# A LoRA kernel: the small matrix A loaded as it lies in DRAM, on the scalar queue, and put in its place by selection matmuls

## The chip, the cores and the metric

The kernel runs on one core of one Trainium2 chip. The metric is device time in microseconds (us) of one execution; lower is better. Executions of the kernel before stayed within about 0.3% in the first runs, so differences of a few tenths of a per cent are hard to tell. A profiled execution gives a span that is about 1.9 us shorter than its time, because the time also holds what lies outside the traced instructions.

## The reference

```python
def setup_inputs():
    batch, seq, d_model, r = 16, 512, 768, 16
    # x: [16, 512, 768], A: [768, 16], B: [16, 768], all float32; scale = 0.5

def reference(x, A, B, scale):
    lora = np.matmul(np.matmul(x, A), B)
    return (x + scale * lora).astype(np.float32)
```

x is 25.2 MB and is read once; the output is 25.2 MB and is written once. A and B are 48 KB each. So nearly all traffic is x and the output, and A and B are a setup matter.

## The kernel before

x is cut into eight groups of 1,024 rows. A group is one load and one store of 3 MB, with 24,576 contiguous bytes on each of 128 partitions. There are six buffers of that size, so the last two loads wait for the first two stores. Each group is cast to 16 bits (ScalarE, "ACT"), transposed in 32x32 blocks (VectorE, "DVE"), multiplied by A (TensorE, "PE"), scaled into a block-diagonal tile (ACT), multiplied by B (PE), and added to x in place (DVE).

A has to stand in a layout that fits the transposed blocks: partition i holds rows 64b + 2i and 64b + 2i + 1 for each of 12 blocks b. The kernel before lets the DMA build that layout, in pieces of 128 bytes. One matmul with `rep` then copies the 32 partitions of A onto four partition quarters.

```python
    def sync_program():
        load(0)                       # ... moved ahead of the opening barrier
        nc.sync.dma_start(
            out=a32.rearrange("i (b r) -> i b r", b=NB),
            in_=A.rearrange("(b i q) r -> i b (q r)", i=Q, q=2),
        ).then_inc(a_in, 16)
        nc.sync.dma_start(out=b32, in_=B).then_inc(b_in, 16)
        for g in range(1, X_BUFS):
            load(g)
        for g in range(NG - 1):
            nc.sync.wait_ge(added, 4 * (g + 1) + 2)
            # ... store group g; after the second store, loads 6 and 7
    # ...
    def vector_program():
        nc.vector.wait_ge(pool_done, 2)
        nc.vector.tensor_copy(out=a16, in_=a32)._wait_ge(a_in, 16).then_inc(setup_dve, 1)
        nc.vector.tensor_copy(out=b16[0:R, :], in_=b32)._wait_ge(b_in, 16).then_inc(setup_dve, 1)
        for a in range(NQ):           # four copies from PSUM into a_diag
            # ...
        nc.vector.tensor_copy(out=b_rep, in_=b_ps)._wait_ge(setup_pe, 2).then_inc(added, 2)
        turn(0, 0, G // 2)._wait_ge(ready, 1)      # the first transpose
        # ...
    def tensor_program():
        nc.tensor.matmul(a_ps, rep, a16, start=True, stop=True)._wait_ge(setup_dve, 1).then_inc(setup_pe, 1)
        # ...
        with nc.tensor.Fori(0, NG) as g:           # the loop over groups
            wait = nc.tensor.lower_val(g + 2)      # waits against a register's value
            # ...
```

## Time and profile before

| | before |
|---|---|
| time, median of 4 runs | 123.52 us (123.25 to 123.57) |
| span of the profiled run | 121.3 us |
| share of the DMA engines' span in use | 97.8% |
| busiest compute engine | DVE, 69% |
| last add ends / last store is issued | 105.6 / 106.1 us |

The page of the kernel before, its rows for the DMA engines: the first row is the busy share of the 16 DMA engines in 40 equal slices of the span, in tenths (9 is 90% or more), the second what they moved, then come the packets and the queue (packets, MB, share of 16 engines).

```profile
DMA  7999999999999999999999999999999999999991
GB/s 227 421 392 419 397 478 413 397 478 421 397 478 405 413 470 413 413 454 430 413 446 438 413 438 446 413 438 438 421 438 438 413 446 438 413 446 438 413 454 73
DMA packets 2736, 50.43 MB, mean 416 GB/s; under 512 B 672, under 2 KB 672, under 8 KB 688
q1 hardware_dynamic: 2736, 50.43, 97.8%
```

No slice between the first and the last has any room. The packet records of the trace say the same: a packet of 24,576 bytes takes 912 ns, so 16 engines stream 431 GB/s. Of the 672 packets under 512 bytes, 384 are A's pieces of 128 bytes and 288 are the completion writes of 18 transfers on 16 engines.

The timeline of the kernel before, DVE's first and last instructions (start us, duration us, engine, line, operation, out<-in, shape, count, idle time before and what ended it):

```profile
10.79 0.35 DVE L175 CAST a_73<-a_70 32x384 f16<-32x384 f32 x1 [10.79 <-DMA a_70<-in_A_dram]
11.10 0.55 DVE L178 CAST b_74<-b_71 16x768 f16<-16x768 f32 x1
11.72 2.26 DVE L183 CAST a_diag<-lora_ps_78 32x384 f16<-32x384 f32 x4
13.99 0.96 DVE L188 CAST b_rep<-lora_ps_79 128x768 f16<-128x768 f32 x1
14.87 3.43 DVE L166 STREAM_TRANSPOSE xt<-xh_66 128x1536 uint32<-128x1536 uint32 x2
...
103.87 1.75 DVE L197 TENSOR_TENSOR x_61<-x_61,lora_ps_79 128x1536 f32<-128x1536 f32 x1
```

The same timeline, the sync queue's issues ("SPq") of the first and the last two stores:

```profile
33.47 0.35 SPq L116 DMA_DIRECT2D out_dram<-x  x1
...
96.11 0.33 SPq L116 DMA_DIRECT2D out_dram<-x  x1
106.12 0.33 SPq L253 DMA_DIRECT2D out_dram<-x_61  x1
```

DVE waits for A until 10.79 us, does the setup, and starts the first transpose at 14.87 us. The chain of waits on the page of the kernel before names DVE as the main part of what ended last:

```profile
DVE 44%; PE 22%; DMA 13%; ACT 6%; SPq 1%; issue 1%
```

That chain is true, and it is still not what bounds the kernel. It ends with the last add; the last store is then issued at 106.12 us, and by the packet records the engines finish the store before it only at 111.7 us (quickest engine) to 112.8 us (slowest). The last store waits in the queue. The two readings differ by the slack that compute has.

### The profile page before, as it was taken

To read this page: it belongs to the slowest core of one execution; us is meant where nothing else is said; L and a number is where in the kernel's file an instruction comes from. 1 tells how busy PE (TensorE), PEld (TensorE's weight loads), DVE (VectorE), ACT (ScalarE), POOL (GpSimd) and SP (SyncE) were. 2 spreads that over 40 slices of the span, in tenths; PEclk is the share of its full clock that TensorE was granted. 3 is DMA by queue.
4 is the path that set the end of the run, shared out by engine and by line. 5 is a ranking of instruction groups with operands and counts; after the bars stand their busy time and mean duration, and the time that the engine had idled before them with its cause. 6 is when DMAs were issued, how large, how long until landed. Compare 5 with 4: busy or idle time off the path is not lost.

```text
span 121.3 us, 888 instructions
## 1 busy us (share of the span) xinstructions
PE 52.1 (43%) x323; PEld 30.6 (25%) x323; DVE 84.2 (69%) x48; ACT 55.9 (46%) x42; POOL 4.9 (4%) x9
## 2 busy tenths in 40 slices
PE   0003109576944684294375449437446745000000
PEld 0000006331622362172144227216213522000000
DVE  0004990299959999999999999999999639800000
ACT  4005929989159719917943395992400220000000
POOL 6900000000000000000000000000000000000000
PEclk9999999965699999999999999999999999975555
DMA  7999999999999999999999999999999999999991
GB/s 227 421 392 419 397 478 413 397 478 421 397 478 405 413 470 413 413 454 430 413 446 438 413 438 446 413 438 438 421 438 438 413 446 438 413 446 438 413 454 73
DMA packets 2736, 50.43 MB, mean 416 GB/s; under 512 B 672, under 2 KB 672, under 8 KB 688
## 3 DMA queue, kind: packets, MB, share of 16 engines
q1 hardware_dynamic: 2736, 50.43, 97.8%
HBM read 25.26 MB, written 25.17 MB: 416 GB/s over the span
## 4 chain that ended last, share of the span: by engine, by line
DVE 44%; PE 22%; DMA 13%; ACT 6%; SPq 1%; issue 1%
DVE xt L166 19%; PE y_ps L224 16%; DMA x_61<-in_x_dram 13%; DVE x_61 L197 8%; DVE x L197 5%; PE lora_ps_79 L238 5%; ACT xh_67 L143 4%; DVE x_65 L197 3%; DVE x_63 L197 3%; DVE x_64 L197 3%; DVE x_62 L197 3%; ACT y_diag L154 1%; PE lora_ps_78 L238 1%; SPq L111 1%; SPq L107 0%
## 5 line engine op out<-in xcount | busy, mean ns | idle before, releaser
L224 PE MATMUL y_ps<-xt,a_diag 128*128 128x256 f16 x192 | 24.8, 287 | 5.8 <-DVE xt L166 5.8
L238 PE MATMUL lora_ps_78<-b_rep,y_diag 128*128 128x512 f16 (+1 forms) x64 | 14.1, 346 | 27.9 <-ACT y_diag L154 14.1
L154 ACT ACTIVATE y_diag<-y_ps 32x256 f16<-32x256 f32 x32 | 12.0, 375 | 28.0 <-PE y_ps L224 27.7
L224 PEld LDWEIGHTS y_ps<-xt,a_diag 128*128 128x128 f16 x192 | 19.3, 101 | 11.6 <-DVE xt L166 6.5
L166 DVE STREAM_TRANSPOSE xt<-xh_67 128x3072 uint32<-128x3072 uint32 x4 | 13.5, 3378 | 5.9 <-ACT xh_67 L143 5.1
L238 PE MATMUL lora_ps_79<-b_rep,y_diag 128*128 128x512 f16 (+1 forms) x64 | 14.4, 351 | 6.1 <-DVE x_61 L197 1.7
L143 ACT CAST xh_66<-x 128x3072 f16<-128x3072 f32 (+1 forms) x3 | 10.7, 3604 | 10.3 <-DMA x<-in_x_dram 10.3
L166 DVE STREAM_TRANSPOSE xt<-xh_66 128x3072 uint32<-128x3072 uint32 (+1 forms) x5 | 13.6, 2728 | 1.8 <-PE y_ps L224 1.8
L238 PEld LDWEIGHTS lora_ps_78<-b_rep,y_diag 128*128 128x128 f16 x64 | 5.1, 100 | 35.8 <-issue 16.6
L143 ACT CAST xh_67<-x_61 128x6144 f16<-128x6144 f32 x2 | 10.6, 5312 | 2.3 <-DMA x_61<-in_x_dram 2.3
L238 PEld LDWEIGHTS lora_ps_79<-b_rep,y_diag 128*128 128x128 f16 x64 | 5.9, 103 | 13.2 <-DVE x_61 L197 2.4
L197 DVE TENSOR_TENSOR x_61<-x_61,lora_ps_78 128x1536 f32<-128x1536 f32 x4 | 7.0, 1741 | 2.8 <-PE lora_ps_78 L238 2.8
L175 DVE CAST a_73<-a_70 32x384 f16<-32x384 f32 x1 | 0.3, 349 | 10.8 <-DMA a_70<-in_A_dram 10.8
L197 DVE TENSOR_TENSOR x_61<-x_61,lora_ps_79 128x1536 f32<-128x1536 f32 x4 | 7.0, 1744 | 0.0
L197 DVE TENSOR_TENSOR x<-x,lora_ps_79 128x1536 f32<-128x1536 f32 x4 | 7.0, 1741 | 0.0
L197 DVE TENSOR_TENSOR x<-x,lora_ps_78 128x1536 f32<-128x1536 f32 x4 | 6.9, 1729 | 0.0
L143 ACT CAST xh_66<-x_62 128x6144 f16<-128x6144 f32 x1 | 5.3, 5313 | 0.4 <-DMA x_62<-in_x_dram 0.4
L143 ACT CAST xh_67<-x_63 128x6144 f16<-128x6144 f32 x1 | 5.3, 5314 | 0.0
L143 ACT CAST xh_67<-x_65 128x6144 f16<-128x6144 f32 x1 | 5.3, 5313 | 0.0
L143 ACT CAST xh_66<-x_64 128x6144 f16<-128x6144 f32 x1 | 5.3, 5312 | 0.0
L209 PE MATMUL lora_ps_78<-a_73,rep 32*128 32x384 f16 x1 | 0.5, 496 | 11.2 <-DVE a_73 L175 11.2
L197 DVE TENSOR_TENSOR x_62<-x_62,lora_ps_79 128x1536 f32<-128x1536 f32 x2 | 3.5, 1742 | 0.0
(23 smaller groups left out, 35.5 us busy)
## 6 DMA issues: line engine op xcount, KB each, us to landing
x<-in_x_dram SPq DMA_DIRECT2D x2, 3072.0 KB, 12.5
x_61<-in_x_dram SPq DMA_DIRECT2D x2, 3072.0 KB, 15.2
out_dram<-x SPq DMA_DIRECT2D x2, 3072.0 KB, 19.1
out_dram<-x_61 SPq DMA_DIRECT2D x2, 3072.0 KB, 15.8
x_62<-in_x_dram SPq DMA_DIRECT2D x1, 3072.0 KB, 22.7
x_63<-in_x_dram SPq DMA_DIRECT2D x1, 3072.0 KB, 29.6
x_64<-in_x_dram SPq DMA_DIRECT2D x1, 3072.0 KB, 36.3
x_65<-in_x_dram SPq DMA_DIRECT2D x1, 3072.0 KB, 43.1
```

The lines of the kernel that those rows point to most:

```text
L111: nc.sync.dma_start(out=b32, in_=B).then_inc(b_in, 16)
L143: i = nc.scalar.copy(out=xh[g % 2][:, rows, :], in_=xs[g % X_BUFS][:, rows, :])
L154: i = nc.scalar.mul(out=y_diag[q, :, q], in_=y_ps[q, :, :], mul=sc)
L166: i = nc.vector.transpose(out=xt[:, rows, :].rearrange("p s w -> p (s w)"), in_=xh[g % 2][:, rows, :].rearrange("p s d -> p (s d)").bitcas ...
L175: nc.vector.tensor_copy(out=a16, in_=a32)._wait_ge(a_in, 16).then_inc(setup_dve, 1)
L197: nc.vector.tensor_tensor(out=rows, in0=rows, in1=lora_ps[n % 2], op=mybir.AluOpType.add)._wait_ge(ups, n + 1).then_inc(added, 1)
L209: nc.tensor.matmul(a_ps, rep, a16, start=True, stop=True)._wait_ge(setup_dve, 1).then_inc(setup_pe, 1)
L224: i = nc.tensor.matmul(y_ps, a_diag[:, k, :], xt_mm[:, :, k // 2, :, k % 2], start=(k == 0), stop=(k == 2 * NB - 1),)
L238: i = nc.tensor.matmul(flat[:, ds(c0, w)], y_diag[:, s + k, :], b_rep[:, ds(c0 - k * D, w)], start=True, stop=True,)
```

## The change

The intent: A should no longer be 384 pieces of 128 bytes in the queue that carries x. It is loaded as it lies in DRAM, with 512 contiguous bytes on each of 96 partitions, and, with B, on the scalar engine's queue, so that neither stands between two loads of x. Four selection matmuls put A's rows in place. The selection matrices are made on GpSimd ("POOL") and by one more matmul.

```diff
@@ sync_program
-        nc.sync.dma_start(
-            out=a32.rearrange("i (b r) -> i b r", b=NB),
-            in_=A.rearrange("(b i q) r -> i b (q r)", i=Q, q=2),
-        ).then_inc(a_in, 16)
-        nc.sync.dma_start(out=b32, in_=B).then_inc(b_in, 16)
@@ pool_program
+        # three memsets and four affine_selects that make wrap, step and mine (cut)
@@ scalar_program
+        nc.scalar.dma_start(
+            out=a32, in_=A.rearrange("(p m q) r -> p m (q r)", m=NM, q=2)
+        ).then_inc(a_in, 16)
+        nc.scalar.dma_start(out=b32, in_=B).then_inc(b_in, 16)
+        nc.scalar.copy(out=sel.rearrange("p m k -> p (m k)"), in_=sel_ps)._wait_ge(
+            setup_pe, 1
+        ).then_inc(setup_act, 1)
@@ vector_program
-        nc.vector.wait_ge(pool_done, 2)
-        nc.vector.tensor_copy(
-            out=a16, in_=a32
+        nc.vector.wait_ge(pool_done, 4)
+        nc.vector.tensor_tensor(
+            out=a16,
+            in0=a32[:, :, None, :].to_broadcast([PA, NM, NB, 2 * R]),
+            in1=mine[:, None, :, None].to_broadcast([PA, NM, NB, 2 * R]),
+            op=mybir.AluOpType.mult,
         )._wait_ge(a_in, 16).then_inc(setup_dve, 1)
@@ tensor_program
-        nc.tensor.matmul(a_ps, rep, a16, start=True, stop=True)._wait_ge(
-            setup_dve, 1
-        ).then_inc(setup_pe, 1)
+        nc.tensor.matmul(
+            sel_ps, wrap, step.rearrange("j m a i -> j (m a i)"), start=True, stop=True
+        )._wait_ge(pool_done, 3).then_inc(setup_pe, 1)
+        nc.tensor.wait_ge(setup_act, 1)
+        for m in range(NM):          # NM = 4
+            i = nc.tensor.matmul(
+                a_ps, sel[:, m, :], a16[:, m].rearrange("p b r -> p (b r)"),
+                start=(m == 0), stop=(m == NM - 1),
+            )
+            # ... the first waits for setup_dve, the last increments setup_pe
```

(Tiles, semaphore numbers and the selects are cut.)

More of the change, by code (lines that the diff above doesn't have):

```diff
@@ L47 @@
     NB = W // Q
+    NM = 4
+    PB, PA = Q // NM, W // NM
+    assert PA <= P and NM * P <= 512
     sc = float(scale)
@@ L58 @@
     y_diag = const.tile([P, G, P], MM_DT, name="y_diag")
-    a32 = const.tile([Q, 2 * NB * R], fp32, name="a32")
+    a32 = const.tile([PA, NM, 2 * R], fp32, name="a32")
+    mine = const.tile([PA, NB], MM_DT, name="mine")
+    wrap = const.tile([PB, PA], MM_DT, name="wrap")
+    step = const.tile([PB, NM, NQ, Q], MM_DT, name="step")
+    sel = const.tile([PA, NM, P], MM_DT, name="sel")
     b32 = const.tile([R, D], fp32, name="b32")
     rep = const.tile([Q, NQ * Q], MM_DT, name="rep")
-    a16 = const.tile([Q, 2 * NB * R], MM_DT, name="a16")
+    a16 = const.tile([PA, NM, NB, 2 * R], MM_DT, name="a16")
     b16 = const.tile([Q, D], MM_DT, name="b16")
@@ L79 @@
     setup_dve, setup_pe = semaphore("setup_dve"), semaphore("setup_pe")
+    setup_act = semaphore("setup_act")
     ready, turned = semaphore("ready"), semaphore("turned")
@@ L128, in pool_program @@
         nc.gpsimd.sem_clear(stored)
-        nc.gpsimd.memset(rep, 0.0).then_inc(pool_done, 1)
+        nc.gpsimd.memset(rep, 0.0)
+        nc.gpsimd.memset(wrap, 0.0)
+        nc.gpsimd.memset(step, 0.0)
+        nc.gpsimd.memset(mine, 1.0).then_inc(pool_done, 1)
         nc.gpsimd.affine_select(
@@ L136, in pool_program @@
         )._wait_ge(pool_done, 1)
+        nc.gpsimd.affine_select(
+            out=wrap.rearrange("j (b k) -> j b k", k=PB),
+            in_=wrap.rearrange("j (b k) -> j b k", k=PB),
+            compare_op=mybir.AluOpType.not_equal, fill=1.0, base=0,
+            pattern=[[0, NB], [-1, PB]], channel_multiplier=1,
+        )
+        nc.gpsimd.affine_select(
+            out=step, in_=step,
+            compare_op=mybir.AluOpType.not_equal, fill=1.0, base=0,
+            pattern=[[1, NM], [0, NQ], [-1, Q]], channel_multiplier=NM,
+        )
+        nc.gpsimd.affine_select(
+            out=mine, in_=mine, compare_op=mybir.AluOpType.is_ge, fill=0.0, base=0,
+            pattern=[[-PB, NB]], channel_multiplier=1,
+        ).then_inc(pool_done, 1)
+        nc.gpsimd.affine_select(
+            out=mine, in_=mine, compare_op=mybir.AluOpType.is_ge, fill=0.0, base=PB - 1,
+            pattern=[[PB, NB]], channel_multiplier=-1,
+        )._wait_ge(pool_done, 2).then_inc(pool_done, 1)
         nc.gpsimd.memset(b16, 0.0)
@@ L162 @@
     b_ps = lora_ps[1][:, 0, :]
+    sel_ps = lora_ps[0].rearrange("p s d -> p (s d)")[0:PA, 512 : 512 + NM * P]
     def turn(g, s0, n):
@@ L186, in vector_program @@
             if a == 0:
-                i._wait_ge(setup_pe, 1)
-        nc.vector.tensor_copy(out=b_rep, in_=b_ps)._wait_ge(setup_pe, 2).then_inc(added, 2)
+                i._wait_ge(setup_pe, 2)
+        nc.vector.tensor_copy(out=b_rep, in_=b_ps)._wait_ge(setup_pe, 3).then_inc(added, 2)
         turn(0, 0, G // 2)._wait_ge(ready, 1)
@@ L208, in tensor_program @@
     def tensor_program():
-        nc.tensor.matmul(a_ps, rep, a16, start=True, stop=True)._wait_ge(
-            setup_dve, 1
-        ).then_inc(setup_pe, 1)
+        nc.tensor.matmul(
[6 more added lines that the diff above has]
+                start=(m == 0), stop=(m == NM - 1),
+            )
+            if m == 0:
+                i._wait_ge(setup_dve, 1)
+        i.then_inc(setup_pe, 1)
         for c0, n in chunks(0, D):
```

## The prediction

> **What bounds the kernel now.** The DMA engines, throughout. The page's DMA row shows 7 tenths in the first of 40 slices, 9 in all others but the last; the queue table says 97.8% for 50.43 MB. In the trace's DMA packet records each 24,576-byte packet takes 912 ns, so 16 engines stream 431 GB/s; 128 packets per engine make 116.7 of the 121.3 us span. The Trainium skill's page "DMA: Bandwidth & Descriptors" (Specifications) gives a fabric ceiling of 435 GB/s; this trace agrees: nothing is left in the rate.
>
> The chain of waits names DVE (44%) and PE (22%), but its last add ends at 105.6 us. The last store is issued at 106.1 us, while the store ahead of it occupies the engines until about 113 (one 3 MB transfer takes 7.3 us). So compute has 6 to 7 us of slack at its end. At the start it has more: the first store is issued at 33.5 us, but the six queued loads end at 47.3.
>
> **What the change does.**
> - DMA: A was 384 packets of 128 B (24 per engine, about 9.4 ns apart: 0.23 us) and becomes 96 of 512 B (6 per engine, estimated 22 ns each: 0.13 us). B is unchanged. The first x packet behind A and B took about 1,200 ns instead of 912 on every engine: 0.29 us, which I read as a stall after small packets. With A and B on a second queue during x_0 it may vanish, or reappear inside x_0. Saving 0.1 to 0.4 us, point 0.3.
> - x_1 and the loads behind it are issued 1.1 us earlier. Worth nothing: x_0 occupies the engines until 9 us.
> - A and B land earlier than their 10.8 and 11.1 us (the same page, on arbitration: each engine round-robins between queue rows by packet; no run shows it yet): I expect 3 to 8 us.
> - POOL gains three memsets and four selects: about 2.4 us (memsets cost about 0.95 ns per column, one 32x128 select 0.30 us), ending at about 8.3 instead of 5.8; DVE waits for it.
> - DVE: the 0.35 us cast of A becomes a 96x1536 multiply, about 1.7 us (the 128x1536 add takes 1.74). PE: one 384-column matmul becomes four, about 1.65 us; the selection matmul and its ACT copy end while x_0 loads.
> - So setup: 8.3 + 1.7 + 1.65 + a_diag 2.26 + b_rep 0.96 = 14.9 us. Before, the first transpose started at 14.87. The new setup work eats the early landing; a win or loss of 2 us would still drown in the slack, because the chain then waits for x_1's landing (18.1 us).
>
> **On the critical path:** only the 0.3 us of queue time.
>
> **Predicted time: 123.25 us, 80% range 122.8 to 123.7.** Faster by over 2%: 0.02; within 2%: 0.95; slower by over 2%: 0.03.
>
> **What would show it.** DMA row 9 in every slice but the first and last; share 97 to 99%; span 120.8 to 121.4; 288 packets under 512 B (the semaphore writes) instead of 672; x_1 landing at 17.6 to 18.2 us; last add ending at 105 to 106; last store about 15 us from issue to landing. The DVE idle of 10.8 us before its first work shrinks to about 8, and ends on POOL rather than A's DMA.
>
> **What would make it wrong.** Two queues that interleave badly (x packets far over 912 ns while both are live). Stores whose start, not the queue, is the limit: then earlier setup would pay more. Setup later by more than 7 us (POOL far slower than estimated): then the last store comes late.

## The result, and the profile after

| | before | after |
|---|---|---|
| time, median of 4 runs | 123.52 us | 123.28 us (123.19 to 123.44) |
| ratio of the fast runs | | 0.9987, 95% interval 0.9969 to 1.0004 |
| span of the profiled run | 121.3 us | 121.6 us |
| A / B usable by DVE | 10.8 / 11.1 us | 11.4 / 13.7 us |
| first transpose starts | 14.9 us | 17.9 us |
| last store issued | 106.1 us | 109.8 us |

Ratios here are the mean time of one kernel's fast runs over that of the other's fast runs of the same rounds, so they are not quite the ratios of the medians. Executions over 1.5% slower than the fastest of the same kernel are left out of the means. The time is the same: the interval contains 1. The profiled run was the slowest of the four (123.44 us); the others had spans of 121.3 and 121.4 us.

The page of the changed kernel, the same rows. There are now two queues, the sync engine's (q1) and the scalar engine's (q10):

```profile
DMA  7999999999999999999999999999999999999990
GB/s 234 407 405 409 437 445 404 445 445 404 445 445 404 445 429 421 396 485 412 396 493 404 404 485 404 412 461 421 429 445 412 437 445 412 437 445 412 445 437 40
DMA packets 2448, 50.43 MB, mean 415 GB/s; under 512 B 288, under 2 KB 384, under 8 KB 400
q1 hardware_dynamic: 2304, 50.33, 97.3%
q10 hardware_dynamic: 144, 0.10, 0.3%
```

A's small pieces are gone (288 packets under 512 bytes, the completion writes), and the DMA row is as full as before. The timeline of the changed kernel, DVE:

```profile
11.44 1.75 DVE L214 TENSOR_TENSOR a_77<-a_70,mine 96x1536 f16<-96x1536 f32 x1 [11.44 <-DMA a_70<-in_A_dram]
13.73 0.55 DVE L220 CAST b_78<-b_75 16x768 f16<-16x768 f32 x1 [0.55 <-DMA b_75<-in_B_dram]
14.74 2.26 DVE L225 CAST a_diag<-lora_ps_82 32x384 f16<-32x384 f32 x4 [0.46 <-PE lora_ps_82 L256]
17.01 0.96 DVE L230 CAST b_rep<-lora_ps_83 128x768 f16<-128x768 f32 x1
17.89 3.43 DVE L205 STREAM_TRANSPOSE xt<-xh_66 128x1536 uint32<-128x1536 uint32 x2
...
107.58 1.75 DVE L239 TENSOR_TENSOR x_61<-x_61,lora_ps_83 128x1536 f32<-128x1536 f32 x1
```

The same timeline, the issues of the first and the last two stores:

```profile
36.65 0.35 SPq L121 DMA_DIRECT2D out_dram<-x  x1
...
99.82 0.33 SPq L121 DMA_DIRECT2D out_dram<-x  x1
109.83 0.33 SPq L304 DMA_DIRECT2D out_dram<-x_61  x1
```

So A was not usable earlier but 0.65 us later, the setup behind it is longer, and every store is issued 3 to 4 us later, without any effect on the time. Why A came late is in the packet records. These are the records of one engine of the changed kernel while both queues are live. The records carry no engine number; the lines were put together by chaining each record to the one whose end it follows, which near-ties can swap.

```
start us   ns    bytes   queue
    4.37   912   24576   sync      a row of x
    5.28    27     512   scalar    A
    5.30   912   24576   sync
    6.21    27     512   scalar    A
    6.24   912   24576   sync
    7.14    27     512   scalar    A
    7.17   912   24576   sync
    8.07    27     512   scalar    A
    8.10   912   24576   sync
    9.01    27     512   scalar    A
    9.03     9       4   sync      x_0 complete
    9.04    27     512   scalar    A
    9.06   912   24576   sync
    9.97     9       4   scalar    A complete
```

The scalar queue gets mostly one small packet for each large packet of the sync queue. A's six packets per engine, and then its completion write, each wait for a turn of 0.9 us. On the slowest engine A's completion write starts at 10.99 us, and DVE starts its multiply 0.45 us after that.

The stores tell how much of the lateness could be afforded. The starts of the completion writes of each transfer in the packet records, on the quickest and on the slowest engine, in us:

```
                    x_1 loaded     x_5 loaded     7th store      last store     last store issued
before            17.0 to 17.6   46.2 to 46.8  111.7 to 112.8  118.9 to 120.0        106.12
after             16.8 to 17.8   46.2 to 47.2  111.6 to 113.2  118.9 to 120.4        109.83
```

### The profile page after: what moved, and what is told of

It reads as the page before. It is cut to its first block, busy times and chain, and to the rows that moved or that the text cites. A ratio compares the mean times of both kernels' runs of the same rounds, so it can differ in the third digit from the quotient of the medians.

```text
span 121.6 us, 908 instructions
## 1 busy us (share of the span) xinstructions
PE 53.3 (44%) x327; PEld 31.3 (26%) x327; DVE 85.6 (70%) x48; ACT 56.5 (46%) x43; POOL 6.8 (6%) x16
## 4 chain that ended last, share of the span: by engine, by line
DVE 51%; PE 28%; DMA 9%; ACT 1%; issue 1%; ACTq 0%; SPq 0%
DVE xt L205 22%; PE y_ps L275 20%; DMA a_70<-in_A_dram 9%; DVE x_61 L239 8%; DVE x L239 5%; PE lora_ps_83 L289 5%; DVE x_63 L239 3%; DVE x_62 L239 3%; DVE x_65 L239 3%; DVE x_64 L239 3%; DVE a_diag L225 2%; DVE a_77 L214 1%; ACT y_diag L192 1%; PE lora_ps_82 L256 1%; DVE b_rep L230 1%
## 5 line engine op out<-in xcount | busy, mean ns | idle before, releaser
L275 PE MATMUL y_ps<-xt,a_diag 128*128 128x256 f16 x192 | 26.0, 296 | 5.9 <-DVE xt L205 5.9
L289 PE MATMUL lora_ps_82<-b_rep,y_diag 128*128 128x512 f16 (+1 forms) x64 | 13.2, 328 | 28.4 <-ACT y_diag L192 13.6
L275 PEld LDWEIGHTS y_ps<-xt,a_diag 128*128 128x128 f16 x192 | 19.9, 104 | 12.2 <-DVE xt L205 6.6
L289 PE MATMUL lora_ps_83<-b_rep,y_diag 128*128 128x512 f16 (+1 forms) x64 | 13.7, 339 | 6.7 <-DVE x_61 L239 1.7
L205 DVE STREAM_TRANSPOSE xt<-xh_66 128x3072 uint32<-128x3072 uint32 (+1 forms) x5 | 13.6, 2728 | 2.3 <-PE y_ps L275 2.3
L214 DVE TENSOR_TENSOR a_77<-a_70,mine 96x1536 f16<-96x1536 f32 x1 | 1.8, 1753 | 11.4 <-DMA a_70<-in_A_dram 11.4
L256 PE MATMUL lora_ps_82<-a_77,sel 96*128 96x384 f16 x4 | 1.5, 521 | 8.9 <-DVE a_77 L214 8.9
```

The lines of the kernel that those rows point to most:

```text
L205: i = nc.vector.transpose(out=xt[:, rows, :].rearrange("p s w -> p (s w)"), in_=xh[g % 2][:, rows, :].rearrange("p s d -> p (s d)").bitcas ...
L214: nc.vector.tensor_tensor(out=a16, in0=a32[:, :, None, :].to_broadcast([PA, NM, NB, 2 * R]), in1=mine[:, None, :, None].to_broadcast([PA, ...
L256: i = nc.tensor.matmul(a_ps, sel[:, m, :], a16[:, m].rearrange("p b r -> p (b r)"), start=(m == 0), stop=(m == NM - 1),)
L275: i = nc.tensor.matmul(y_ps, a_diag[:, k, :], xt_mm[:, :, k // 2, :, k % 2], start=(k == 0), stop=(k == 2 * NB - 1),)
L289: i = nc.tensor.matmul(flat[:, ds(c0, w)], y_diag[:, s + k, :], b_rep[:, ds(c0 - k * D, w)], start=True, stop=True,)
```

## The experiments

Twelve kernels were run. As a rule of safety, semaphore waits in new kernels were against constants, so TensorE's loop over the eight groups, whose waits are against a register's value, was written out in all of them. That needed its own controls, and comparisons are made within this family: against the written-out kernel before (`u_before`) or the written-out changed kernel (`u_after`). Kernels of one call share a chip and the runs of the kernel before. There were three calls on three chips: the two controls with `old_on_act` and `new_on_sp`; the delays with `early_ab`; and the last four. So the later two groups are compared with the controls through their ratios to the kernel before. The ratios use the fast runs of the rounds, which leaves out the profiled execution. The medians take in all executions, slow ones too; all executions were fast but one of `delay_4`, one of `delay_8` and three of `old_on_act`.

| run | time, median | ratio to the kernel before, 95% interval |
|---|---|---|
| u_before | 124.57 | 1.0075 (1.0053 to 1.0098) |
| u_after | 124.12 | 1.0053 (1.0034 to 1.0072) |
| new_on_sp | 124.45 | 1.0070 (1.0048 to 1.0091) |
| old_on_act | 135.86 (fast run: 133.41) | 1.1041 (1.0983 to 1.1098), from slow runs; the fast run alone about 1.079 |
| delay_2 | 124.24 | 1.0047 (1.0022 to 1.0073) |
| delay_4 | 125.37 | 1.0105 (1.0058 to 1.0152) |
| delay_8 | 128.36 | 1.0364 (1.0304 to 1.0425) |
| early_ab | 124.08 | 1.0048 (1.0024 to 1.0071) |
| no_ab | 124.07 | 1.0060 (1.0033 to 1.0086) |
| no_b | 124.05 | 1.0050 (1.0024 to 1.0077) |
| b_wide | 124.20 | 1.0072 (1.0046 to 1.0099) |
| a_five | 127.02 | 1.0304 (1.0281 to 1.0326) |

**Theory 1**: the DMA engines bound the time from start to end, and compute has a slack of a few us, in which the later setup drowns. **Rival**: the time follows compute (as the chain of waits suggests), and a saving in the loads and a loss in the setup happened to cancel.

### The controls: u_before and u_after

```diff
-        with nc.tensor.Fori(0, NG) as g:
-            wait = nc.tensor.lower_val(g + 2)
+        for g in range(NG):
+            wait = g + 2
```

(and the same for the other two waits of the loop)

> Control: the kernel before with TensorE's loop of eight groups written out, so that its waits are against constants; nothing else changed. Every theory expects a ratio of 0.998 to 1.002 to the kernel before, A and B landing at 10.8 and 11.1 us, first transpose at about 14.9 us, last store issued at about 106 us.

> Control: the changed kernel with the same loop written out. Expected like the changed kernel: ratio 0.997 to 1.000, A landing at about 11.4 us and B at about 13.7 us on the second queue, one 512-byte packet of A between two 24,576-byte packets of x on each engine, first transpose at about 17.9 us, last store issued at about 109.8 us.

Both were correct. The expectation of an unchanged time failed: writing out the loop cost 0.5 to 0.75%. The page of `u_before` shows a kind of traffic that the page of the kernel before does not have:

```profile
q1 hardware_dynamic: 2736, 50.43, 96.9%
q8 instruction: 2, 0.03, 0.1%
```

The two instruction packets have 16,384 bytes and took 1.06 and 0.97 us, at 45.7 and 76.7 us. Each sits on one engine. In the records of `u_before` the slowest engine falls from 1.0 us to 2.0 us behind the quickest at the first of them, and is 2.5 us behind at the end (119.1 to 121.6 us), where it was 1.1 us behind in the kernel before. So about 1 us of foreign work on one of 16 engines showed up as about 1 us of time. That is by itself a sign of how full these engines are, and it says that the slowest engine ends the kernel. The attribution rests on these records; no run took the fetches away alone.

In everything else the controls repeat their originals within 0.7 us: first transpose at 15.18 and 17.71 us, last store issued at 106.75 and 109.87 us. The written-out change is 0.22% below the written-out original (1.0053 against 1.0075), with overlapping intervals.

### old_on_act: the old 128-byte pieces on the scalar queue

```diff
 sync_program
-        nc.sync.dma_start(out=a32..., in_=A.rearrange("(b i q) r -> i b (q r)", i=Q, q=2))
-        nc.sync.dma_start(out=b32, in_=B)
 scalar_program
+        nc.scalar.dma_start(out=a32..., in_=A.rearrange("(b i q) r -> i b (q r)", i=Q, q=2))
+        nc.scalar.dma_start(out=b32, in_=B)
```

> The kernel before with its old 128-byte loads of A, and B, on the scalar queue; nothing else. Theory 1 (the second queue gets one packet per engine for each 24,576-byte packet of x, and compute has a slack of a few us only): A's 24 packets per engine take 24 times 0.92 us from 5.3 us on, A lands at about 28 to 29 us, the first transpose starts at about 34 us, the slack is used up, and the time is 134 to 141 us (ratio 1.09 to 1.14). Rival 2 (the engines are busy whatever compute does, a late A costs nothing): 123.3 to 123.6 us, ratio 1.00. Rival 3 (the second queue's packets go in bursts, A late for another reason such as completion latency): A lands by 13 us, ratio 1.00.

The median is 135.86 us, but three of the four executions count as slow (over 1.5% above the quickest), and no fast one was left for the ratio. The one fast execution, which is the profiled one, took 133.41 us, about 9.8 us or 7.9% over the kernel before. That is just below the 134 to 141 us of Theory 1 and far from the two rivals. The timeline of `old_on_act`, DVE's start:

```profile
26.41 0.35 DVE L175 CAST a<-a 32x384 f16<-32x384 f32 x1 [26.41 <-DMA a<-in_A_dram]
28.76 0.55 DVE L178 CAST b<-b 16x768 f16<-16x768 f32 x1 [2.01 <-DMA b<-in_B_dram]
...
32.38 3.43 DVE L166 STREAM_TRANSPOSE xt<-xh 128x1536 uint32<-128x1536 uint32 x2
```

The same run, stretches of 2 us (columns: stretch, length, busy time and count of PE, PEld, DVE, ACT and POOL, granted PE clock, DMA share, GB/s):

```profile
44.00:46.00 2.00, 0.57 (x4) 0.31 (x4) 2.00 (x2) 2.00 (x1) 0.00 (x0) 1.00 0.97 418
46.00:48.00 2.00, 1.16 (x9) 0.62 (x8) 2.00 (x2) 1.22 (x1) 0.00 (x0) 1.00 0.06 25
48.00:50.00 2.00, 2.00 (x21) 1.71 (x19) 2.00 (x2) 0.00 (x0) 0.00 (x0) 1.00 0.00 0
```

The same 48 KB, on the second queue but in 24 packets per engine instead of 6, arrive at 26.4 us: their first packets start at 5.4 us and their last at 25.0 us, again about one packet per row of x. This is the turn-taking of Theory 1, and it excludes that A's late arrival in the changed kernel is a matter of completion latency. The slack is then used up: all six loads are done by 47.1 us, no store is ready, and the DMA engines stand idle until the first store's packets start at 51.2 us. They stand idle once more before the second store, from 58.9 to 61.5 us. The second half of the change (512 bytes per partition) is what makes the first half (the second queue) bearable.

### new_on_sp: the new form, but on the sync queue behind x_0

```diff
 scalar_program
-        nc.scalar.dma_start(out=a32, in_=A.rearrange("(p m q) r -> p m (q r)", m=NM, q=2))
-        nc.scalar.dma_start(out=b32, in_=B)
 sync_program, behind load(0)
+        nc.sync.dma_start(out=a32, in_=A.rearrange("(p m q) r -> p m (q r)", m=NM, q=2))
+        nc.sync.dma_start(out=b32, in_=B)
```

> The changed kernel's load form, selection matmuls and setup, but A and B issued on the sync queue behind x_0 as before. Theory 1: A lands at about 10.6 us and B at about 10.9, setup is about 2.5 us longer than before, so the first transpose starts at about 17.2 us, a little earlier than in the changed kernel and 2.3 us later than before; ratio 0.997 to 1.000. Rival (the separate queue is what gave the small gain): ratio 1.000 or above.

The landing and the setup were as expected: DVE's multiply starts at 10.77 us and the first transpose at 17.22 us. The time, 124.45 us and a ratio of 1.0070, lies between the two controls and cannot be told from either. For the new form, which queue A and B are on has no visible effect on the time.

### delay_2, delay_4, delay_8: compute made later on purpose

```diff
         nc.vector.tensor_copy(out=b_rep, in_=b_ps)...
+        for k in range(n):               # n = 2, 4 or 8, in the changed kernel
+            nc.vector.tensor_copy(out=pad, in_=b_ps)._wait_ge(padded, k).then_inc(padded, 1)
         turn(0, 0, G // 2)._wait_ge(ready, 1)
```

> The changed kernel, loop written out, with two extra chained copies of 768 columns (about 1.0 us each) on VectorE before its first transpose: all compute 2.0 us later. Theory 1 (the DMA engines bound the time, compute has a slack): in the written-out changed kernel the last store was issued at 109.87 us; the first engine ended the store before at 111.7 us, the last at 113.8 us, and a store took 0.83 us from issue to its first packet where it was waited for; so slack is 1.0 us for the quickest engine and 3.1 us for the slowest, which ends the kernel. Time 124.0 to 124.5 us, last store issued at 111.9. Rival (the time follows compute, and the change lost by its later setup what it won elsewhere): 126.1 us.

> The same with four extra copies, compute 4.0 us later. Theory 1: the last store is issued at about 113.8 us, 0.9 us past the slowest engine's need: time 124.6 to 125.6 us. Rival (time follows compute): 128.1 us. Second rival (slack of 6 to 7 us, as estimated from the kernel before): 124.1 us.

> The same with eight extra copies, compute 8.0 us later. Theory 1: slack of 3.1 us used up, the rest shows one for one: 128.3 to 129.7 us, and the DMA row shows an idle stretch. Rival (time follows compute): 132.1 us. Second rival (slack of 6 to 7 us): 125 to 126 us.

The last issue of the sync queue in `u_after`, in `delay_2`, and then in `delay_4`:

```profile
109.87 0.33 SPq L304 DMA_DIRECT2D out_dram<-x  x1
```

```profile
111.77 0.33 SPq L308 DMA_DIRECT2D out_dram<-x  x1
```

```profile
114.01 0.33 SPq L308 DMA_DIRECT2D out_dram<-x  x1
```

| | last store issued later than in u_after by | time over u_after (difference of the ratios, in us) |
|---|---|---|
| delay_2 | 1.9 us | -0.1 us |
| delay_4 | 4.1 us | +0.6 us |
| delay_8 | 8.2 us | +3.8 us |

The rival expected 2, 4 and 8 us. The first two us cost nothing (-0.1 us, to about 0.4 us either way by the intervals), so the time does not follow compute. The delay of 8 us does show, with 3.8 us. The fast runs of `delay_8` took 127.32, 127.50 and 129.22 us (mean 128.0), two of them below the range that Theory 1 gave and none near the other two; the executions of `delay_4` and `delay_8` spread over 2 to 3 us.

Theory 1 had the size about right and the place wrong. It expected the time to be lost at the last store. The profile of `delay_8` (a slow run, so only its issue times and idle stretches are read) has the idle stretch before the second store. Its issue of that store, and its stretches of 2 us:

```profile
56.70 0.34 SPq L123 DMA_DIRECT2D out_dram<-x  x1
```

```profile
52.00:54.00 2.00, 1.16 (x8) 0.57 (x7) 2.00 (x2) 1.53 (x1) 0.00 (x0) 1.00 0.55 234
54.00:56.00 2.00, 2.00 (x20) 1.66 (x18) 2.00 (x2) 0.00 (x0) 0.00 (x0) 1.00 0.03 8
56.00:58.00 2.00, 0.90 (x9) 0.53 (x6) 1.74 (x2) 1.04 (x3) 0.00 (x0) 1.00 0.47 197
```

The engines end the first store at 53.3 to 54.1 us, and the second one's packets start at 57.5 us: 3.4 us idle on the slowest engine. After that everything on the engines is later too, and the last store (issued at 118.08 us) comes in time for the slowest engine, which ends the store before at 119.0 us. In `delay_4` no store came too late for the slowest engine. Its profiled execution, 1.4 us longer than that of `u_after`, has 1.7 us more per engine in rows of x that took over 912 ns, nearly all of it between 55 and 80 us; why is open. So the delays show that compute has a slack of at least about 2 us and of less than 8, and not how large it is at the last store.

### early_ab: A and B issued together with x_0

```diff
 scalar_program
-        nc.scalar.dma_start(out=a32, ...)
-        nc.scalar.dma_start(out=b32, in_=B)
 ahead of the opening barrier, where load(0) is
+        nc.scalar.dma_start(out=a32, ...)
+        nc.scalar.dma_start(out=b32, in_=B)
```

(the new allocation of the two tiles, which that place needs, is cut)

> The changed kernel, loop written out, with A and B issued from the scalar queue before the opening barrier, at the same time as x_0. A's six packets per engine should interleave with x_0's from the start and land at 7 to 9 us instead of 11.3, the first transpose start at 14.4 to 16 us instead of 17.7, the last store be issued at 106.5 to 108 us. Theory 1 (compute has slack): time 123.8 to 124.4 us, like the written-out changed kernel (124.12). Rival (the late setup of the changed kernel cost something): 2 us less, 122 us.

124.08 us, like `u_after`, but the test was weaker than planned, because A hardly came earlier: the last store is issued at 109.54 us instead of 109.87. The timeline of `early_ab`:

```profile
10.93 1.75 DVE L223 TENSOR_TENSOR a<-a,mine 96x1536 f16<-96x1536 f32 x1 [10.93 <-DMA a<-in_A_dram]
...
17.39 3.43 DVE L214 STREAM_TRANSPOSE xt<-xh 128x1536 uint32<-128x1536 uint32 x2
```

Its first packets of A run at 3.5 us instead of 5.2, behind two rows of x instead of four. But the last start at 9.2 us on the slowest engine, and the completion write takes a turn of its own, up to 10.3 us. The expectation of 7 to 9 us had left out that turn and the slowest engine. So this run does not tell whether an earlier setup would pay.

### no_ab: neither A nor B is loaded (wrong result)

```diff
-        nc.sync.dma_start(out=a32..., in_=A...)
-        nc.sync.dma_start(out=b32, in_=B)
+        nc.gpsimd.memset(a32, 0.0).then_inc(a_in, 16)
+        nc.gpsimd.memset(b32, 0.0).then_inc(b_in, 16)
```

> Wrong result on purpose: the kernel before, loop written out, loads neither A nor B; both tiles are set to zero by GpSimd. It bounds what any change of A's and B's loads can win. Theory 1 (only their time on the engines counts: 24 packets at 9.4 ns, one B packet of 121 ns, and about 0.29 us by which the next x packet is longer, together 0.65 us per engine): x_1's landing 0.6 us earlier, time 0.3 to 0.8 us below the written-out kernel before (124.57): 123.8 to 124.3 us. First transposes start at about 13.2 us rather than 15.2, worth nothing more. Rival (setup is on the path): 2 us or more below, 122.5 us or less.

124.07 us, a ratio of 1.0060: 0.15% below `u_before`, about 0.2 us, with overlapping intervals. The setup is now done at 11 us and the first transpose starts at 13.28 us instead of 15.18. But compute keeps little of that: the second transpose waits for x_1's cast and starts at 23.11 us instead of 23.70, and the last store is issued at 106.32 us instead of 106.75. So this run cannot tell either whether earlier compute would pay. What it does show is that A's and B's loads are worth some tenths of a us, so there is no saving of 3 us in them that could hide the cost of a setup 3 us later. The cast of x_1 starts at 17.76 us instead of 18.36, so the 0.6 us of queue time were indeed won at that point. But they did not reach the end. The same stretch in `no_ab`, and then in `u_before`:

```profile
44.00:45.00 1.00, 1.00 (x11) 0.73 (x8) 0.90 (x1) 0.00 (x0) 0.00 (x0) 1.00 1.27 369
45.00:46.00 1.00, 0.13 (x2) 0.00 (x0) 0.83 (x1) 0.81 (x3) 0.00 (x0) 1.00 0.54 147
```

```profile
44.00:45.00 1.00, 1.00 (x11) 0.85 (x10) 1.00 (x1) 0.00 (x0) 0.00 (x0) 1.00 0.91 393
45.00:46.00 1.00, 0.56 (x6) 0.24 (x3) 0.74 (x2) 0.39 (x2) 0.00 (x0) 1.00 0.93 385
```

In `no_ab` the last packets of the sixth load took 1.0 to 2.3 us instead of 0.91, just before the first store, and the first store's first packets start at 46.1 us in both. The gain was given back there. Why the change from loads to stores was slow in this execution is not settled: only one execution of each kernel has records, and the excess over 912 ns per row, summed over the stretch that holds this change, varied between kernels from about 0.1 to 1.0 us per engine without a pattern that the runs explain.

### no_b and b_wide: what makes the rows of x behind A and B slow (wrong results on purpose)

```diff
 no_b
-        nc.sync.dma_start(out=b32, in_=B).then_inc(b_in, 16)
+        nc.gpsimd.memset(b32, 0.0).then_inc(b_in, 16)
 b_wide (and b32 set to zero)
-        nc.sync.dma_start(out=b32, in_=B).then_inc(b_in, 16)
+        nc.sync.dma_start(out=b_wide, in_=B.rearrange("r (a k) -> (r a) k", k=96)).then_inc(b_in, 16)
```

> Wrong result on purpose: as the kernel before, loop written out, with A's 128-byte packets but no B. It tells which load makes the x packets behind A and B last about 1,200 ns instead of 912. If small packets do (as the prediction read it), the first x packets of x_1 still last 1,100 to 1,200 ns and the time is 0.1 us below the written-out kernel before. If B does (as the changed kernel's trace suggests, where x packets between A's 512-byte packets last 912 ns and those behind B 1,110 to 1,220), they last about 912 ns and the time is about 0.4 us below: 124.1 us.

> Wrong result on purpose: as the kernel before, loop written out, but B's 48 KB lands as 384 bytes on each of 128 partitions instead of 3,072 bytes on 16, in a tile that nothing reads; zeros take B's place. If landing on 16 partitions makes the long x packets, they fall to 912 to 960 ns behind it, and the time is 0.1 to 0.3 us below the written-out kernel before. If B's bytes or the switch of source do it, they stay at 1,100 to 1,200 ns and the time stays.

The packet records, rows of x that start from 9 to 16.5 us:

```
             rows over 1,050 ns   their median   time over 912 ns each, per engine
u_before            16               1,169 ns          0.35 us
no_b                 1               1,093 ns          0.16 us
b_wide               1               1,080 ns          0.12 us
```

So the rows over 1,050 ns come with B's 16 packets of 3,072 bytes on 16 partitions, not with A's small packets: with A's 384 small packets still there and B as 128 packets of 384 bytes on 128 partitions all but one are gone. A's small packets are not without effect: 0.16 and 0.12 us per engine remain, and in `no_ab`, with neither load, 0.00. (`b_wide` changes the partitions and the size of the packets together, so which of the two it is stays open.) This corrects a reading of the prediction for the larger part of the stall. Their worth does not show in the time: 1.0050 and 1.0072 against 1.0075, with overlapping intervals. Part of it came back later, up to 46 us: rows there took 0.27 and 0.30 us per engine over 912 ns each, against 0.13 in `u_before`. Both expectations of a time gain are unconfirmed.

### a_five: A's pieces four times more

```diff
         nc.sync.dma_start(out=a32..., in_=A...).then_inc(a_in, 16)
+        for c in range(4):
+            nc.sync.dma_start(out=a_more[:, c, :]..., in_=A...).then_inc(more, 16)
```

(a wait for these loads, ahead of load 6, is cut)

> The kernel before, loop written out, loads A's 384 packets of 128 bytes four times more behind the first, in tiles that nothing reads. Theory 1 (each nanosecond on the engines shows in the time): 96 more packets per engine at 9.4 ns, 0.90 us, plus up to 0.29 us more if small packets cause a stall of their own: the second x lands 0.9 to 1.2 us later and the time is 125.3 to 125.9 us. Rival (small packets hide behind other work): 124.6 us.

127.02 us: 2.3% over `u_before`, about 2.8 us, where 0.9 to 1.2 us were expected. Neither Theory 1 nor the rival had this. The timeline of `a_five`, the sync queue's issues:

```profile
1.38 6.34 SPq L114 DMA_DIRECT2D a_more<-in_A_dram  x4
7.77 2.21 SPq L118 DMA_DIRECT2D b<-in_B_dram  x1
10.02 2.88 SPq L96 DMA_DIRECT2D x<-in_x_dram  x5
```

The issues of so many small pieces held the sync engine, and x_1 was issued at 10.02 us instead of 2.20, when x_0 was already in. So the engines ran dry: the stretches from 9 to 11 us moved only 152 and 140 GB/s, and the first rows of x_1 took about 1.65 us. A further 0.9 us per engine came at the change from loads to stores, as in `no_ab`. The run was meant to measure the cost of a packet and instead measured a queue that was not filled in time, so it does not give that cost and decides between neither.

## Why the prediction was right, and where it was not

1. **The bound was read right.** The DMA row is as full after as before. Compute made 2 us later does not show in the time, and made 8 us later it shows with 3.8 us. The rival, that time follows compute, is refuted by `delay_2`. Its other half, that a saving in the loads cancelled a loss in the setup, is refuted by `no_ab`: taking both loads away wins about 0.2 us, where some 3 us would have to cancel.
2. **The time was right**: 123.25 us predicted, 123.28 measured, within 2%.
3. **The gain of 0.3 us is not shown.** The ratio of 0.9987 has an interval that contains 1, and 0.9978 between the two controls is no firmer. The landing of x_1 did not move as predicted: its cast starts at 18.30 us against 18.09 before. Removing both loads altogether measured about 0.2 us, with overlapping intervals. The agreement of the point values to 0.03 us is luck. The records of the profiled executions say why little was to be had: most of the 0.3 us was the stall, and that came back behind B on the other queue (rows of x that start from 9 to 16.5 us took 0.33 us per engine over 912 ns each, before and after). The prediction had named this possibility. What is left is A's own time, 24 packets 9.4 ns apart before, and 6 after, each of which put off the next row by about 24 ns: 0.23 and 0.14 us, an estimated saving of about 0.09 us.
4. **The landing of A and B was wrong.** "I expect 3 to 8 us" became 11.4 and 13.7. The queues do alternate, but the second one gets about one packet of 512 bytes per row of x on each engine, not a batch. `old_on_act` confirms it at four times the packet count.
5. **The setup was therefore wrong**: 14.9 us predicted, 17.9 measured. The term that failed is its start: POOL ended at 7.8 us and was not waited for, A's DMA was. The other terms held: multiply 1.75 us (1.7 predicted), four matmuls 1.46 (1.65), a_diag 2.26, b_rep 0.96. B's later landing cost nothing more: its cast ended at 14.28 us, before the matmuls that a_diag waited for.
6. **"Last add ending at 105 to 106" was wrong**: 109.3 us. The prediction assumed that the chain waits for x_1 in any case. With A at 11.4 us it waits for the setup: the second transpose starts at 26.61 us, behind the first matmuls, and not at 23.43 behind x_1's cast. The last store then needed 11.8 us from issue to the end of the span, not 15.
7. **The slack was a little smaller than said, and the last store is not the only place for it.** With 0.83 us from an issue to its first packet (measured where the engines were idle: issued at 111.77, first packet at 112.60 us in `delay_2`), the slowest engine's need left about 112.8 - 0.83 - 106.12 = 5.9 us before and 113.2 - 0.83 - 109.83 = 2.5 us after. Both are estimates. Each store has a slack of its own, by the same working: that of the second store, issued at 44.75 and 48.45 us, was 8.5 us before and 5.2 us after, and `delay_8` ran short there first. The change thus spent more than half of the slack at the last store and bought nothing visible with it.
8. **The stall was for the most part put down to the wrong load**: to small packets, where `no_b` and `b_wide` show that the larger part of it (0.35 us per engine with both loads, 0.16 with A alone) belongs to B's load in its form of 16 packets on 16 partitions.

What stays open: how large the slack is at the last store (no run measured it apart from the other stores), why rows are longer in the delayed runs, the pause at the change from loads to stores, what it is in B's form that makes the next rows long, and whether the change is worth 0.0 or 0.3 us. No run gave a version that beats both kernels clearly; with 116.7 us of row packets in a span of 121.3 us, and about 0.2 us won without both loads, A and B have nothing larger to give.

## What to carry to other kernels

When the chain of waits ends well before the last store's data move, measure the slack at the stores (queue free minus issue) before costing any change to compute or setup, and at every store, since here the second ran short before the last; delaying compute on purpose is a cheap proof that there is a slack, and its trace shows where it ends. Here a second DMA queue did not let small transfers overtake large ones: beside a queue of 24 KB packets each small packet waited about 0.9 us for its turn, so what must arrive early needs few packets per engine or a place at the front. And a change that leaves the time alone can still spend slack, so compare issue times and not only totals.

## What the Trainium skill lacked or had wrong

- "DMA: Bandwidth & Descriptors", section on queues, rings and completion order: it says that an engine takes turns between queue rows by packet, and gives about 9 to 17 descriptors as typical for a packet. Here the turn was mostly one record of 512 or 128 bytes per 24,576-byte record (whether a record of the trace is one descriptor or a whole packet in the page's sense, no run shows); six A records took from 5.28 to 9.04 us on one engine, and 24 took until 25.0 us. The page does not say that a small transfer beside large descriptors is slowed in this way, nor that the completion write takes a turn of its own.
- The same page, Specifications: the ceiling of 435 GB/s for one core agrees with this trace (24,576 bytes in 912 ns on 16 engines, 431 GB/s). Its first-byte latency of about 0.6 us for this path can't be held against a number of ours, since the row doesn't say from where it counts: a store's first packet on idle engines came 0.83 to 0.84 us after the start of its issue and 0.50 us after the end of it.
- "Trainium Kernel Development and Optimization", Key Constraints: that queues of several engines share the same 16 DMA engines, so that a second one saves issue time only, agrees in the time with `u_after` against `new_on_sp` (1.0053 and 1.0070, overlapping). It did cost something in landing: B was usable at 13.6 us on the second queue and by 11.1 us on the first.
- "Runtime: NRT & Kernel Launch", the section on instruction fetch, has fetches in blocks of 16 KiB and what they cost the fetching engine; it lacks what they cost the transfers of a kernel bound by DMA. Here two packets of 16,384 bytes, about 1 us each on one DMA engine, came with 0.5 to 0.75% more time.
- No page has the slowing of large packets behind a load of 16 packets of 3,072 bytes on 16 partitions (it would belong to "SBUF — State Buffer", beside the bandwidth of a load by the ports that its own partitions reach): 1,169 ns instead of 912 for the next row on each engine, all but gone when the same bytes come as 128 packets on 128 partitions.
